# A delta-rule block for the latents alone with unsplit float32 operands, the context still in high and low parts

## The chip, the cores and the metric

The kernel runs on one core of a Trainium2 chip. The metric is device time in microseconds of one execution, the median of several runs. The core's engines are TensorE (PE, matmuls; its weight loads are listed as PEld), VectorE (DVE), ScalarE (ACT), GpSimd (POOL) and SyncE (SP), whose queue issues nearly all DMAs. A core works with one on-chip memory of 128 partitions (SBUF) and with accumulators (PSUM) in banks of 512 float32 columns.

## The reference

Two blocks run on 256 tokens of width 1024 (x). The first mixes stick-breaking attention with a state-space branch, then attends to a memory, then applies a convolutional feed-forward layer. The second has two layers; each is a mixer followed by a mixture of 32 experts. The mixer of its first layer is the one of this case, a gated delta rule that runs in both directions, with 8 heads of 128:

```
p = h @ w_in                      # h = modulate(x) of the latents, or of the context (256 tokens)
q, k, v = split(silu(conv3(p[:, :3072])));  z = p[:, 3072:4096]
beta = sigmoid(p[:, 4096:4112]);  g = -exp(a_log) * softplus(p[:, 4112:] + dt_bias)
per chunk of 64 tokens:           # u, w solve a unit lower triangular system built from k, beta, g
    v_new = u - w @ S;  o = q_dec @ S + (q k^T * decay) @ v_new;  S = S * g_last + k_dec^T @ v_new
y = (norm(o) * silu(z)) @ w_out   # the latents' scan starts from the context's final S
```

The context needs only its final states S, so it has no q and no z. h is a norm: x times its inverse root mean square, times a column of scales, plus a column of shifts. All inputs and the output are float32.

## The kernel before

Activations are kept transposed, features on partitions and the 256 tokens in the free dimension, as 8 slices of 128 features. A weight tile is 1 MB (128 x 2048 float32) and holds 256 output columns for all 8 slices, so two output blocks of 128 columns. `wload` (line 312) loads it on the SP queue into a ring of five.

Matmuls of the dense projections are made of three products in a faster float32 form that rounds its operands (F32R). `split` (line 321) turns half a weight tile into a high part (ScalarE copy, line 325) and a low part (subtract, line 327, on VectorE, or on GpSimd where a share says so; the shares of the latents' queries, values and gates say GpSimd every time, that of the keys VectorE). There are two buffers for such pairs (`wsp`). The activation h is kept as a high and a low part as well (hh, hl). `mm3` (line 330) issues high x high, high x low and low x high. `gemm_t` (line 336) does this for all blocks of a projection: 24 matmuls a block, and then an `evac` that empties the bank. Attention scores (line 835), the recurrence, the expert layers and the transposes use plain float32 operands with no split.

`mod_t` (line 941) makes h: squares on ScalarE, the inverse root on VectorE or GpSimd, two matmuls a slice with a diagonal of it (line 504, transposing), then per slice an affine step on VectorE (952), a ScalarE copy to hh (953) and a VectorE subtract to hl (954).

The class `Delta` holds the steps for the context (dc) and for the latents (dl). `decays` (1030) projects beta and g from a 128 x 8 x 32 weight that is loaded and split once near the start (lines 1486 to 1491), and builds masks on GpSimd and VectorE. `keys` (1138), `values` (1173) and `queries` (1192) are projections with a convolution on VectorE (`conv3`, 993, its steps at lines 997, 998 and 1002) behind each block. `chunks` (1205) forms k k^T, sends it through DRAM to regroup it, inverts 32 x 32 triangles in a loop of 31 x 2 dependent VectorE operations (1237, 1239), sends the result through DRAM again and joins the parts with small matmuls (1264, 1275). `steps` (1300) is the recurrence: four steps of matmuls and VectorE updates. The gates z (1635) are projected in two halves, the second of them behind the recurrence (`Z_LATE`), and the output projection `wa_out` follows, then the experts.

The order of the work is written by generators. `weave` (239) runs several of them beside one another, the latents (1583), the context (1399), queries, values and gates (1616), the two `decays`, and the modulation weights of line 910; each `yield` gives a cost in planned microseconds, and the generator with the least planned time goes on. The framework then orders each engine's instructions by priority and by a timeline of its own; on the chip each engine, and the SP queue, works strictly in that order.

Of the kernel before, what the change touches and what calls it, by code (L numbers as in the profile page):

```python
# [12 lines left out]
F32R = mybir.dt.float32r  # L13
# [194 lines left out]
def tile_blocks(ctx: ExitStack, tc: tile.TileContext, A, out):  # L208
# [121 lines left out]
    def mm3(ps, ah, al, bh, bl, start, stop):  # L330
# [2 lines left out]
        PE.matmul(ps, ah, bl, start=False, stop=False)  # L333
        PE.matmul(ps, al, bh, start=False, stop=stop)  # L334

    def gemm_t(name, tiles, kt, h, evac, share=None):


        hh, hl = h
        late = None  # L340
        ncols = WT // kt
        cb = 1024 // (kt * P)
        blk = 0
        for i in tiles:
            w3 = wload(name, i).rearrange("p (k n) -> p k n", n=ncols)
            for n0 in range(0, ncols // P, cb):
                h3, l3 = split(w3[:, :, n0 * P:(n0 + cb) * P], (kt, cb * P), SHARES.get(name, 0) if share is None else share)
                for j in range(cb):
                    ps = bank()[:, :T]
                    for k in range(kt):  # L350
                        mm3(ps, h3[:, k, j * P:(j + 1) * P], l3[:, k, j * P:(j + 1) * P], hh[:, k], hl[:, k],
                            k == 0, k == kt - 1)
                    later = evac(blk, ps)
                    if late:
                        late()
                    late = later if callable(later) else None
                    blk += 1
                yield 2.6
        if late:
            late()  # L360

    def gemm_n(name, i, ncols, h, pss, k0, klast):


        hh, hl = h
        nh = ncols // 512
        w2 = wload(name, i).rearrange("p (k n) -> p k n", n=ncols)
        kc = 2 // nh
        for ka in range(0, WT // ncols, kc):
            h3, l3 = split(w2[:, ka:ka + kc], (kc, ncols), SHARES.get(name, 0))  # L370
            for k in range(kc):
                kk = k0 + ka + k
                for t in range(2):
                    ah, al = hh(kk, t), hl(kk, t)
                    for n in range(nh):
                        sl = slice(n * 512, (n + 1) * 512)
                        PE.matmul(pss[t][n], ah, h3[:, k, sl], start=kk == 0, stop=False)
                        PE.matmul(pss[t][n], ah, l3[:, k, sl], start=False, stop=False)
                        PE.matmul(pss[t][n], al, h3[:, k, sl], start=False, stop=kk == klast)  # L379
            yield 2.6  # L380

    def gemm_out(name, h, nh=2, evac=None):


        f = [lambda k, t, q=q: q[:, k, t * P:(t + 1) * P] for q in h]
        pss = [[None] * nh, [None] * nh]
        for n in range(nh):
            if evac and n and n == nh - 1:
# [11 lines left out]
        for c in range(2):  # L400
            ps = [bank("acc")[:, :256] for t in range(2)]
            for kq in range(2):
                h3, l3 = split(ws[kq][:, :, c * 256:(c + 1) * 256], (4, 256), SHARES.get(name, 0))
                for k in range(4):
                    for t in range(2):
                        kk = 4 * kq + k
                        ah, al = f[0](kk, t), f[1](kk, t)
                        PE.matmul(ps[t], ah, h3[:, k], start=kk == 0, stop=False)
                        PE.matmul(ps[t], ah, l3[:, k], start=False, stop=False)
                        PE.matmul(ps[t], al, h3[:, k], start=False, stop=kk == 7)  # L410
                yield 2.6
# [529 lines left out]
    def mod_t(src, a, b, E=G, wait=6, mark=None):  # L941

        with urgent():
            dg = diagonals(rms(src, E))
        hh = big("hh", (8, T), F32R)
        hl = big("hl", (8, T), F32R)
        have[mark] = True
        yield wait
        for k in range(8):
            ps = transposed(src, dg, k)  # L950
            t = temp()
# [4 lines left out]
        return hh, hl  # L956

    def gated_into(x, gb, router):

# [53 lines left out]
    class Delta:  # L1013
# [16 lines left out]
        def decays(self):  # L1030
            yield from until(("h", self.live))
            use(*DECB)
            hh, hl = self.h
            dth = self.dth
            E = G if DEC_POOL & (2 if self.live else 1) else V
            M = G if MASK_POOL & (2 if self.live else 1) else V
            pb = bank()
            for k in range(8):
                mm3(pb[:32, :T], wsh[:, k], wsl[:, k], hh[:, k], hl[:, k], k == 0, k == 7)
            bs = temp()[:32]  # L1040
            for t in range(2):
                S.activation(bs[:, t * P:(t + 1) * P].rearrange("p (c j) -> p c j", j=64), in_tile(pb[:32, :T], t), AF.Copy)
# [440 lines left out]
    nexp = const.tile([P, 16], F32, name="nexp")  # L1483
    exp_cols(nexp, rows32[:, 0:16], 16)
    V.tensor_scalar(nexp, nexp, -1.0, None, op0=OP.mult)
    wsm = temp().rearrange("p (k n) -> p k n", n=32)
    nc.sync.dma_start(wsm, A["wa_s"])
    wsh = const.tile([P, 8, 32], F32R, name="wsh")
    wsl = const.tile([P, 8, 32], F32R, name="wsl")
    S.activation(wsh, wsm, AF.Copy)  # L1490
    V.tensor_tensor(wsl, wsm, wsh, op=OP.subtract)

    class ExpertWeights:


# [87 lines left out]
    def latents():  # L1583
        yield from first()
        have["ffn"] = True
        use("mm", "acc", "fb", "acc")
        dl.h = yield from mod_t(x, scale_col("norm_mix0", ada_c0, 1, 0), ada_c0[:, 0, :, 0], V if RS_V & 4 else G, WAIT3, "x3")
        have["h", True] = True
        use(*KEYB)
        yield from dl.keys()  # L1590
# [411 lines left out]
```

## Time and profile before

| | |
|---|---|
| median of 3 runs | 2170.59 us (2167.99 to 2180.1) |
| the profiled execution | 2169.38 us |
| its span, first to last instruction | 2167.6 us, 31109 instructions |
| mean granted TensorE clock | 0.964 of full speed |
| delta rule of the latents | about 713 to 990 us of the span |

The profile is one execution. A page gives each engine's busy time, queries give stretches, lines and single instructions in order of time. Times of rows are microseconds from the start of the span unless marked ns. A matmul's own duration includes the way through the array, so the cost of one in a series is read from the distance of the starts.

### The profile page before, as it was taken

How to read it: one execution, taken by the hardware profiler on the slowest of the kernel's cores; microseconds unless marked ns; L12 is line 12 of the kernel's file. 1: busy time of each engine (PE TensorE's matmuls, PEld its weight loads, DVE VectorE, ACT ScalarE, POOL GpSimd, SP SyncE). 2: the span in 40 equal slices, each digit the busy share in tenths (PEclk: the TensorE clock that was granted, in tenths of full speed). 3: DMA queues.
4: the chain of work that ended last, by engine and by line, in shares of the span. 5: the costliest groups of instructions: out<-in, count | busy, mean ns of one | idle time of the engine just before them, and what ended most of it. 6: DMA issues, size and time to landing. Idle time of an engine off the chain costs nothing. (4 is left out here: it accounts for less than half of the span.)

```text
span 2167.6 us, 31109 instructions
## 1 busy us (share of the span) xinstructions
PE 1976.3 (91%) x12476; PEld 1269.3 (59%) x12476; DVE 1107.4 (51%) x2277; ACT 652.4 (30%) x1236; POOL 289.0 (13%) x444
## 2 busy tenths in 40 slices
PE   5999999989999889898999989898798999999996
PEld 5778787789988767777434333333596333333332
DVE  6797377867966587666333222222565332222223
ACT  4325655555645332543111011110342111111101
POOL 6484001110000374320000000000000000000000
PEclk8999999999999888998999999999898999999999
DMA  6533355536555235548799999997754999999992
GB/s 260 195 114 120 137 214 185 214 128 219 198 173 203 101 139 182 182 176 332 281 420 419 419 413 386 404 373 286 294 203 179 408 420 419 420 384 418 419 391 98
DMA packets 103508, 592.08 MB, mean 273 GB/s; under 512 B 30272, under 2 KB 30656, under 8 KB 32704
## 3 DMA queue, kind: packets, MB, share of 16 engines
q1 hardware_dynamic: 103216, 589.52, 69.6%
q8 instruction: 100, 1.64, 0.3%
q10 hardware_dynamic: 144, 0.52, 0.1%
q14 instruction: 48, 0.39, 0.0%
HBM read 585.81 MB, written 4.19 MB: 272 GB/s over the span
## 5 line engine op out<-in xcount | busy, mean ns | idle before, releaser
L327 DVE TENSOR_TENSOR whl<-w,whl 128x1024 fp32r<-128x1024 f32 x210 | 267.0, 1272 | 123.8 <-ACT whl L325 122.1
L1802 PE MATMUL acc<-wa,xq 128*64 128x512 f32 x1152 | 311.7, 599 | 2.6 <-DVEq L1873 2.6
L325 ACT ACTIVATE whl<-w 128x1024 fp32r<-128x1024 f32 x236 | 248.2, 1054 | 168.3 <-PE acc L379 72.8
L332 PE MATMUL mm<-hh,whl 128*128 128x256 f32 x912 | 264.9, 291 | 15.7 <-DVE hl L524 5.3
L334 PE MATMUL mm<-hh,whl 128*128 128x256 f32 x912 | 264.2, 290 | 1.5 <-DVE whl L327 1.3
L333 PE MATMUL mm<-hl,whl 128*128 128x256 f32 x912 | 260.9, 286 | 0.0
L332 PEld LDWEIGHTS mm<-hh,whl 128*128 128x128 f32 x912 | 177.0, 194 | 24.5 <-issue 7.3
L1802 PEld LDWEIGHTS acc<-wa,xq 128*64 128x64 f32 x1152 | 93.2, 137 | 163.3 <-issue 156.3
L334 PEld LDWEIGHTS mm<-hh,whl 128*128 128x128 f32 x912 | 177.0, 194 | 10.9 <-issue 4.4
L1802 PE MATMUL acc<-w,xq 128*64 128x512 f32 x640 | 182.8, 597 | 0.0
L333 PEld LDWEIGHTS mm<-hl,whl 128*128 128x128 f32 x912 | 176.9, 194 | 1.2 <-issue 0.4
L1841 DVE TENSOR_TENSOR acc<-acc,gb 128x512 f32<-128x512 f32 x64 | 44.7, 699 | 172.0 <-PE acc L1837 144.2
L1849 DVE TENSOR_TENSOR x<-x,mm 128x512 f32<-128x512 f32 x128 | 82.3, 683 | 95.8 <-PE mm L1848 95.8
L1802 PEld LDWEIGHTS acc<-w,xq 128*64 128x64 f32 x640 | 54.3, 137 | 86.8 <-issue 83.2
L1783 DVE TENSOR_SCALAR xq<-mm,scnorm_ffn,ada_c 128x256 f32<-128x256 f32 x64 | 34.4, 543 | 128.2 <-PE mm L1781 67.6
L332 PE MATMUL acc<-hh,whl 128*128 128x256 f32 x288 | 86.7, 301 | 4.5 <-DVE x L547 3.8
L334 PE MATMUL acc<-hh,whl 128*128 128x256 f32 x288 | 84.9, 295 | 0.3 <-DVE whl L327 0.2
L1784 ACT ACTIVATE xq<-mm,ada_c,scnorm_ffn 128x256 f32<-128x256 f32 x64 | 35.6, 563 | 161.9 <-DVE xq L1783 154.4
L1695 POOL MEMSET t2b<- 128x512 f32 x1 | 0.5, 524 | 627.9 <-PE fb L1570 627.9
L333 PE MATMUL acc<-hl,whl 128*128 128x256 f32 x288 | 84.2, 292 | 0.0
L327 POOL TENSOR_TENSOR whl<-w,whl 128x1024 fp32r<-128x1024 f32 x26 | 62.6, 2412 | 129.0 <-ACT whl L325 64.9
L1837 PE MATMUL acc<-wa,t2a 128*64 128x512 f32 x288 | 77.7, 598 | 2.3 <-ACT t2a L1827 1.2
(796 smaller groups left out, 3852.1 us busy)
## 6 DMA issues: line engine op xcount, KB each, us to landing
wa<-in_w_dram SPq DMA_DIRECT2D x216, 1024.0 KB, 10.5
w<-in_w_dram SPq DMA_DIRECT2D x120, 1024.0 KB, 9.5
w<-in_ada_w_dram SPq DMA_DIRECT2D x48, 1024.0 KB, 4.9
ww<-in_w_dram SPq DMA_DIRECT2D x48, 1024.0 KB, 10.4
w<-in_w_up_dram SPq DMA_DIRECT2D x22, 1024.0 KB, 4.8
w<-in_wa_kv_dram SPq DMA_DIRECT2D x16, 1024.0 KB, 4.9
w<-in_wb_in_dram SPq DMA_DIRECT2D x12, 1024.0 KB, 4.8
w<-in_w_down_dram SPq DMA_DIRECT2D x11, 1024.0 KB, 4.9
```

The costliest lines, as they stand in the source:

```text
L325: S.activation(h3, src, AF.Copy)
L327: (G if share and nsplit[0] % share == 0 else V).tensor_tensor(l3, src, h3, op=OP.subtract)
L332: PE.matmul(ps, ah, bh, start=start, stop=False)
L333: PE.matmul(ps, ah, bl, start=False, stop=False)
L334: PE.matmul(ps, al, bh, start=False, stop=stop)
L1695: G.memset(beats, 0.0)
L1783: V.tensor_scalar(xt[:, k0], ps[:, 0], a[:, k0:k0 + 1], b[:, k0:k0 + 1], op0=OP.mult, op1=OP.add)
L1784: S.activation(xt[:, k0 + 1], ps[:, 1], AF.Identity, scale=a[:, k0 + 1:k0 + 2], bias=b[:, k0 + 1:k0 + 2])
L1802: PE.matmul(ph[i][sl], xt[:, 4 * kq + k, s0 + 64 * e:s0 + 64 * e + 64], w[e][:, k * 512:(k + 1) * 512], start=kq == 0 and k == 0, stop=kq ...
L1837: PE.matmul(py[c][sl], ht[:, f, sl], w[e][:, f * 512:(f + 1) * 512], start=f == 0, stop=f == 3, tile_position=(0, 64 * e))
L1841: V.tensor_tensor(py[c][:m], py[c][:m], gb[:m, cs], op=OP.mult)
L1849: V.tensor_tensor(x[:, t, cs], x[:, t, cs], pa, op=OP.add)
```

## The change

For the latents alone, h stays one float32 tensor `hf`, written from the transposing matmul by VectorE and ScalarE in turn; `gemm_t` gets whole operands and issues 8 plain float32 matmuls a block with the weight as loaded, no split. Keys, values, queries and gates of the latents take this way, and their decays. The context keeps hh and hl and its split weights. The small decay weight is loaded inside each `decays` (for the context it is split there). `gemm_n` and `gemm_out` get the same branch, which nothing here takes: the output projection keeps its split. In the planned order a step of an unsplit projection counts 3.4 instead of 2.6, a slice of the norm 0.8 instead of 1.

```diff
+    def whole(h):
+        return not isinstance(h, (tuple, list))
 def gemm_t(name, tiles, kt, h, evac, share=None):
         for i in tiles:
             w3 = wload(name, i).rearrange("p (k n) -> p k n", n=ncols)
+            if whole(h):
+                for j in range(ncols // P):
+                    ps = bank()[:, :T]
+                    for k in range(kt):
+                        PE.matmul(ps, w3[:, k, j * P:(j + 1) * P], h[:, k], start=k == 0, stop=k == kt - 1)
+                    later = evac(blk, ps)
+                    if late:
+                        late()
+                    late = later if callable(later) else None
+                    blk += 1
+                    if (j + 1) % cb == 0:
+                        yield 3.4
+                continue
+            hh, hl = h
...
 def mod_t(src, a, b, E=G, wait=6, mark=None, exact=False):
+        if exact:
+            hf = big("hf", (8, T))
...
         for k in range(8):
             ps = transposed(src, dg, k)
+            if exact:
+                if k % 2:
+                    V.tensor_scalar(hf[:, k], ps, a[:, k:k + 1], b[:, k:k + 1], op0=OP.mult, op1=OP.add)
+                else:
+                    S.activation(hf[:, k], ps, AF.Identity, scale=a[:, k:k + 1], bias=b[:, k:k + 1])
+                yield 0.8
+                continue
...
 def decays(self):
+            wsm = temp().rearrange("p (k n) -> p k n", n=32)
+            nc.sync.dma_start(wsm, A["wa_s"])
+            if not self.live:
+                wsh, wsl = temp(F32R).rearrange("p (k n) -> p k n", n=32), temp(F32R).rearrange("p (k n) -> p k n", n=32)
+                S.activation(wsh, wsm, AF.Copy)
+                V.tensor_tensor(wsl, wsm, wsh, op=OP.subtract)
             for k in range(8):
-                mm3(pb[:32, :T], wsh[:, k], wsl[:, k], hh[:, k], hl[:, k], k == 0, k == 7)
+                if self.live:
+                    PE.matmul(pb[:32, :T], wsm[:, k], self.h[:, k], start=k == 0, stop=k == 7)
+                else:
+                    mm3(pb[:32, :T], wsh[:, k], wsl[:, k], self.h[0][:, k], self.h[1][:, k], k == 0, k == 7)
...
-    wsm = temp().rearrange("p (k n) -> p k n", n=32)
-    nc.sync.dma_start(wsm, A["wa_s"])
-    wsh = const.tile([P, 8, 32], F32R, name="wsh")
-    wsl = const.tile([P, 8, 32], F32R, name="wsl")
-    S.activation(wsh, wsm, AF.Copy)
-    V.tensor_tensor(wsl, wsm, wsh, op=OP.subtract)
...
-        dl.h = yield from mod_t(x, scale_col("norm_mix0", ada_c0, 1, 0), ada_c0[:, 0, :, 0], V if RS_V & 4 else G, WAIT3, "x3")
+        dl.h = yield from mod_t(x, scale_col("norm_mix0", ada_c0, 1, 0), ada_c0[:, 0, :, 0], V if RS_V & 4 else G, WAIT3, "x3", True)
```

## Rows read from the trace of the kernel before

**Rows 1.** The page's totals: busy us (share of the span) xinstructions.
```profile
PE 1976.3 (91%) x12476; PEld 1269.3 (59%) x12476; DVE 1107.4 (51%) x2277; ACT 652.4 (30%) x1236; POOL 289.0 (13%) x444
```
**Rows 2.** Stretches: from:to length, busy PE PEld DVE ACT POOL (x), clock, DMA, GB/s.
```profile
735.00:798.00 63.00, 63.00 (x543) 51.61 (x532) 51.67 (x140) 27.62 (x72) 43.36 (x104) 0.95 0.46 170
798.00:840.00 42.00, 34.31 (x289) 28.58 (x286) 29.23 (x70) 11.12 (x19) 26.75 (x33) 0.84 0.48 150
840.00:882.00 42.00, 36.11 (x311) 29.02 (x310) 39.88 (x104) 15.50 (x34) 12.77 (x6) 0.92 0.52 186
882.00:914.00 32.00, 27.55 (x432) 25.92 (x430) 14.05 (x29) 15.78 (x31) 13.90 (x6) 0.95 0.71 212
914.00:965.00 51.00, 51.00 (x676) 39.67 (x674) 33.94 (x103) 22.04 (x71) 7.94 (x5) 1.00 0.48 187
...
1050.00:1500.00 450.00, 417.71 (x1946) 161.89 (x1942) 126.72 (x223) 51.75 (x90) 0.00 (x0) 1.00 0.98 405
```
**Rows 3.** Timeline of TensorE, 690 to 1000: start, us, line, out<-in, count.
```profile
689.98 0.28 PE L332 MATMUL mm<-hh,whl 128*128 128x256 f32 x1
...
692.86 0.28 PE L332 MATMUL mm<-hh,whl 128*128 128x256 f32 x1
...
733.95 1.92 PE L910 MATMUL fb<-w,cst 128*32 128x512 f32 x16
```
**Rows 4.** Line 835 (count, duration ns min/median/max, first and last start, forms).
```profile
L835 PE MATMUL acc<-kx,qx x32: 378/379/382, 407.0 to 417.3; 128*128 128x256 f32 x32
```
**Rows 5.** Timeline of TensorE, 407 to 418.
```profile
407.05 3.62 PE L835 MATMUL acc<-kx,qx 128*128 128x256 f32 x16
410.50 0.60 PE L917 MATMUL fb<-ident,t2b 128*128 128x128 f32 x4
```
**Rows 6.** Groups by line, 713 to 990: busy, mean ns, idle before.
```profile
L327 POOL TENSOR_TENSOR whl<-w,whl 128x1024 fp32r<-128x1024 f32 x25 | 60.3, 2414 | 98.6 <-ACT whl L325 64.9 <-PE mm L1390 30.9 <-issue 2.7
...
L327 DVE TENSOR_TENSOR whl<-w,whl 128x1024 fp32r<-128x1024 f32 x7 | 10.8, 1540 | 0.5 <-ACT whl L325 0.5
...
L325 ACT ACTIVATE whl<-w 128x1024 fp32r<-128x1024 f32 x32 | 33.5, 1051 | 4.0 <-DMA w<-in_wa_q_dram 2.7 <-DMA w<-in_wa_z_dram 1.3
```
**Rows 7.** Timeline of GpSimd, 840 to 900.
```profile
863.79 2.41 POOL L327 TENSOR_TENSOR whl<-w,whl 128x1024 fp32r<-128x1024 f32 x1 [2.40 <-ACT whl L325]
```
**Rows 8.** Timeline of VectorE, 840 to 900: first, two inner and last inverse steps.
```profile
840.82 0.20 DVE L1237 TENSOR_TENSOR t1a<-inva 128x31 f32<-128x31 f32 x1 [3.14 <-DMA inva<-da]
...
862.25 0.42 DVE L1239 TENSOR_TENSOR inva<-inva,t1a 128x252 f32<-128x252 f32 x1
...
863.88 2.59 DVE L1239 TENSOR_TENSOR inva<-inva,t1a 128x247 f32<-128x247 f32 x1
...
881.50 0.19 DVE L1239 TENSOR_TENSOR inva<-inva,t1a 128x31 f32<-128x31 f32 x1
```
**Rows 9.** Timeline of VectorE, 713 to 735, the norm.
```profile
726.59 0.54 DVE L952 TENSOR_SCALAR t1a<-acc,scnorm_mix,ada_c 128x256 f32<-128x256 f32 x1
...
728.41 0.76 DVE L954 TENSOR_TENSOR hl<-t1a,hh 128x256 fp32r<-128x256 f32 x2 [0.94 <-ACT hh L953]
```
**Rows 10.** Timeline of TensorE, 796 to 812: the wait stands in brackets.
```profile
806.53 1.97 PE L1352 MATMUL fb<-t2b,ti 64*64 64x128 f32 x16 [5.50 <-DVE t2b L1344]
...
809.16 3.35 PE L910 MATMUL fb<-w,cst 128*32 128x512 f32 x16
```
**Rows 11.** Timeline of VectorE, 793 to 807.
```profile
793.87 1.99 DVE L1307 TENSOR_TENSOR dm<-dec,m 128x16 f32<-128x16 f32 x1
...
800.72 2.88 DVE L1314 COPY se<-eg 64x16 f32<-64x16 f32 x4
```
**Rows 12.** Timeline of VectorE, 968 to 992.
```profile
973.20 2.23 DVE L1608 TENSOR_TENSOR sso<-sso,so 128x16 f32<-128x16 f32 x1 [0.82 <-ACT t1a L1604]
...
980.64 3.38 DVE L327 TENSOR_TENSOR whl<-w,whl 128x1024 fp32r<-128x1024 f32 x1
```
**Rows 13.** DMA issues of the whole span: count, KB each, median us to landing.
```profile
t1a<-in_wa_s_dram SPq DMA_DIRECT2D x1, 128.0 KB, 11.1
```

More of the change, by code (lines that the diff above doesn't have):

```diff
@@ L334, in mm3 @@
         PE.matmul(ps, al, bh, start=False, stop=stop)
+    def whole(h):
+        return not isinstance(h, (tuple, list))
     def gemm_t(name, tiles, kt, h, evac, share=None):
-        hh, hl = h
         late = None
@@ L362, in gemm_n @@
     def gemm_n(name, i, ncols, h, pss, k0, klast):
-        hh, hl = h
         nh = ncols // 512
@@ L368, in gemm_n @@
         kc = 2 // nh
+        if whole(h):
+            for k in range(WT // ncols):
+                kk = k0 + k
+                for t in range(2):
+                    for n in range(nh):
+                        PE.matmul(pss[t][n], h(kk, t), w2[:, k, n * 512:(n + 1) * 512], start=kk == 0, stop=kk == klast)
+                if (k + 1) % kc == 0:
+                    yield 3.4
+            return
+        hh, hl = h
         for ka in range(0, WT // ncols, kc):
@@ L382, in gemm_out @@
     def gemm_out(name, h, nh=2, evac=None):
-        f = [lambda k, t, q=q: q[:, k, t * P:(t + 1) * P] for q in h]
+        if whole(h):
+            f = lambda k, t: h[:, k, t * P:(t + 1) * P]
+        else:
+            f = [lambda k, t, q=q: q[:, k, t * P:(t + 1) * P] for q in h]
         pss = [[None] * nh, [None] * nh]
@@ L402, in gemm_out @@
             for kq in range(2):
+                if whole(h):
+                    for k in range(4):
+                        for t in range(2):
+                            kk = 4 * kq + k
+                            PE.matmul(ps[t], f(kk, t), ws[kq][:, k, c * 256:(c + 1) * 256], start=kk == 0, stop=kk == 7)
+                    yield 3.4
+                    continue
                 h3, l3 = split(ws[kq][:, :, c * 256:(c + 1) * 256], (4, 256), SHARES.get(name, 0))
@@ L939, in scale_col, with mod_t @@
         return a
-    def mod_t(src, a, b, E=G, wait=6, mark=None):
+    def mod_t(src, a, b, E=G, wait=6, mark=None, exact=False):
         with urgent():
             dg = diagonals(rms(src, E))
-        hh = big("hh", (8, T), F32R)
-        hl = big("hl", (8, T), F32R)
+        if exact:
+            hf = big("hf", (8, T))
+        else:
+            hh = big("hh", (8, T), F32R)
+            hl = big("hl", (8, T), F32R)
         have[mark] = True
@@ L950, in mod_t @@
             ps = transposed(src, dg, k)
+            if exact:
+                if k % 2:
+                    V.tensor_scalar(hf[:, k], ps, a[:, k:k + 1], b[:, k:k + 1], op0=OP.mult, op1=OP.add)
+                else:
+                    S.activation(hf[:, k], ps, AF.Identity, scale=a[:, k:k + 1], bias=b[:, k:k + 1])
+                yield 0.8
+                continue
             t = temp()
@@ L955, in mod_t @@
             yield 1
-        return hh, hl
+        return hf if exact else (hh, hl)
     def gated_into(x, gb, router):
@@ L1032, in decays @@
             use(*DECB)
-            hh, hl = self.h
             dth = self.dth
@@ L1036, in decays @@
             M = G if MASK_POOL & (2 if self.live else 1) else V
+            wsm = temp().rearrange("p (k n) -> p k n", n=32)
[4 more added lines that the diff above has]
+                V.tensor_tensor(wsl, wsm, wsh, op=OP.subtract)
             pb = bank()
             for k in range(8):
-                mm3(pb[:32, :T], wsh[:, k], wsl[:, k], hh[:, k], hl[:, k], k == 0, k == 7)
+                if self.live:
+                    PE.matmul(pb[:32, :T], wsm[:, k], self.h[:, k], start=k == 0, stop=k == 7)
+                else:
+                    mm3(pb[:32, :T], wsh[:, k], wsl[:, k], self.h[0][:, k], self.h[1][:, k], k == 0, k == 7)
             bs = temp()[:32]
```

## The prediction

> **What bounds the kernel now.** I read the page's totals first, then one table of stretches, then single engines inside the stretch that the change touches. The totals [rows 1] show TensorE busy 91% of the span and VectorE 51%, but a share over the whole span says nothing of one stage. The table [rows 2] does. From 1050 to 1500 us (the first expert stage) the DMA engines are 0.98 busy at 405 GB/s: that stage lasts as long as its weights take to arrive, starts when the work before it is done, and so passes a shift on one to one. I assume the same of what follows it. The change acts before, from 713 us (norm of the latents) to 990 us (output projection of the delta rule). There TensorE reads 63.00 of 63 and 51.00 of 51 us in two stretches, yet 34.31 of 42, 36.11 of 42 and 27.55 of 32 in the three between, while VectorE has 39.88 of 42 in 840 to 882. The reader is to see two kinds of stretch: those packed with matmuls, where each microsecond added to TensorE is lost, and 798 to 914, where TensorE waits and a VectorE chain (the triangular inverses, 62 dependent operations at lines 1237 and 1239) sets the pace.
>
> **TensorE pays more.** A block here is one 128-column output block of a projection: 24 matmuls of split operands, at lines 332 to 334. Two of them 24 apart start at 689.98 and 692.86 [rows 3], so a block takes 2.88 us, 0.120 a matmul. The unsplit form stands at line 835: plain float32, 128x128 stationary, 256 columns, just the shape that is added. Its trace has 32 records [rows 4] for 16 matmuls in the code (four heads, two tiles, two k), so a float32 matmul leaves two records. Sixteen records run from 407.05 to the next start at 410.50 [rows 5]: 0.216 us each, 0.431 a matmul. A block of 8 takes 3.45 us, 0.57 more than before. Keys, values, queries and gates have 8 blocks each: 32 x 0.57 = 18.2 us. The decays have 32 stationary columns; no row shows float32 at this shape. At line 835's price they go from at most 24 x 0.120 = 2.88 to 3.45, +0.57; at one pass each they would take 8 x 0.120 = 0.96, a gain of 1.9. I take the nearer row, +0.6, and leave both ends in the range. TensorE thus gets 19 us more.
>
> The Trainium skill would price this step higher: "FP8 and Floating Point Precision", section "TensorE Precision Notes", counts four passes for true float32, and "TensorE: Matmul & The Clock Gate", section "Back-to-back issue gap", gives 256/2.4 + 2.5 = 109 ns a pass. By them a block would go from 24 x 0.109 = 2.62 to 32 x 0.109 = 3.49 us, +0.87, and the sum over 32 blocks would be 28 us. The four passes agree with 0.431 [rows 5], the 0.109 does not agree with the 0.120 [rows 3].
>
> **The other engines get time back.** In 713 to 990 the splits of these weights are 24 of the 25 on GpSimd at 2.41 us (values, queries, gates), six on VectorE for the keys (two more ran before) at 1.23 us ((7 x 1.540 - 3.38)/6, without the one of [rows 12]), and 32 on ScalarE at 1.05 us [rows 6]; one or two rows belong to the output projection and stay. The larger return is indirect. While GpSimd runs a split, VectorE operations that read SBUF stand still: the split from 863.79 to 866.20 [rows 7] lies on a VectorE subtract that takes 2.59 us, where its neighbour of almost the same size takes 0.42 [rows 8]. In the stretch of the inverse loop there are five such, from 843.6 to 875.8, each 1.7 to 2.2 us above the time of its neighbours: 10.1 us.
>
> **The sum, stage by stage.**
> (a) Norm. Today each slice needs a VectorE affine step, a ScalarE copy and a VectorE subtract; the last subtract ends at 728.41 + 0.76 = 729.2, the last affine step at 726.59 + 0.54 = 727.1 [rows 9]. One affine step is left, on two engines in turn; I take 0.54 for either. With no subtracts ahead of it in the queue the last ends near 726.4 (an estimate: 727.1 less two of the subtracts, 0.76 together), 2.8 us sooner; the 0.6 of the decays comes behind it. -2.3, bounds 0 and -4.
> (b) Keys and first two query blocks, 735 to 798. TensorE is contiguous; nine blocks lie here: 9 x 0.57 = +5.1. VectorE gives back 5 x 1.23 = 6.2 us, but TensorE shows no gap for it; I take 2 of it, nearer to the rows of TensorE. +3.1, bounds -1.1 and +5.1.
> (c) 798 to 840. TensorE waits 5.50 us for a VectorE step of the context's recurrence [rows 10]. Ahead of that step stand small operations that splits hold up: line 1307 takes 1.99 and the four at line 1314 take 2.88 [rows 11], where a step of this size takes 0.2 [rows 8]: 1.8 + 2.1 = 3.9 us. The next weight product of line 910 then runs below full clock (the stretch has 0.84 [rows 2]), 3.35 us [rows 10] against the 1.92 of the same form at 733.95 [rows 3]: 1.4 more. Against it six query blocks, +3.4. -1.9, bounds +3.4 and -5.3.
> (d) The inverses, 840 to 882. -10.1; the five blocks inside lie under the VectorE chain. Without that cover they would cost 2.9. Bounds -4 and -11.
> (e) 882 to 914. From the last inverse step at 881.50 [rows 8] the result goes to DRAM and back. Nothing in this trip changes. Eight blocks of values and gates lie here, +4.6, half of them under the trip: +2.3, bounds 0 and +4.6.
> (f) The recurrence, 914 to 965, keeps its instructions: 0, if no more gate blocks land in it than today (none).
> (g) End, 965 to 990. Line 1608 takes 2.23 instead of 0.2, and line 327 3.38 instead of 1.23 [rows 12], with the last gate step behind it: both lie under GpSimd splits of the gates. -4.2, against it +0.7 for four gate blocks that now fill today's waits. -3.5, bounds 0 and -6.
> (h) The context keeps its splits, but the small decay weight (128 KB) is now loaded at each use, and its split of about 1 us follows the load. Ahead of the context's decays nothing hides it but the queue's lead. A load of this tensor took 11.1 us [rows 13]; SP works in order, and behind it stand weight loads that are mostly early. +1, bounds 0 and +11. For the latents the load lies under the norm.
> Sum: -2.3 + 3.1 - 1.9 - 10.1 + 2.3 + 0 - 3.5 + 1 = -11.4. The profiled execution took 2169.4 us (2167.6 of span, 1.8 around it), 1.2 below the median of the three runs; 2169.4 - 11.4 gives 2158.
>
> A weight tile now goes back to the ring when its last matmul has read it, not after its split, up to one block (3.45 us) later. The loads still lead by four tiles, so I count nothing; if that cover is gone, the landing of a tile shows as a TensorE gap. The order of the emitted work also shifts: a block counts 3.4 units in it instead of 2.6.
>
> **Rivals.**
> *TensorE is the bound all along.* Every added 19 us is paid and the VectorE time returned becomes waiting; only (a) stays: 2169.4 + 19 - 2.3 = 2186. It decides once no stretch between 735 and 990 has a TensorE gap. For it: the two full stretches. Against it: 18.0 us in which TensorE is idle in 798 to 914 (7.7 + 5.9 + 4.4 [rows 2]), the longest wait of them for VectorE [rows 10]. 0.16.
> *The gates slip into the recurrence.* Values end later than the inverses in the emitted order, so the four gate blocks that fill the trip today land in 914 to 965, where TensorE is full: 4 x 3.45 = 13.8. 2158 + 13.8 - 2.3 of (e) = 2170, no change. For it: values are emitted 6.4 units later per projection. Against: TensorE is idle in the trip if they don't run there. 0.27.
> *VectorE is the bound in (b) too.* Then 6.2 instead of 2 comes back; with (c) at its lower end: 2158 - 4.2 - 3.4 = 2150. For it: 51.67 of 63 us VectorE busy there. Against it: 63.00 of 63 on TensorE. 0.17.
> *The pages' price.* 0.30 a block more than my rows on 32 blocks, all on the path: 2158 + 9.6 = 2168; 0.02, for its 0.109 is not what the trace has.
> That the change doesn't do what it says (an unsplit matmul that is no slower) is excluded by the shape of line 835.
>
> **How the numbers follow.** Forecast 2158: 0.38. A measurement of this kernel tells apart about 0.5%, 11 us either way. My forecast lies just beyond that edge (12.6 below the median), so I give 0.28 of it, and all of the 0.17 at 2150, to faster, with 0.03 of the slip coming out lower: 0.48. Slower are the TensorE bound's 0.16 and 0.02 of the slip: 0.18. The rest, 0.34, is no change. One case in ten left out at either end gives 2141 to 2183; the forecast's own range is 2149 to 2168.
>
> **What would show it.** Blocks of 16 records over 3.45 us; no GpSimd split but the output projection's one or two; inverse loop near 31 us from first to last step instead of 40.7; no 5.5 us TensorE gap ahead of line 1352; line 1608 near 0.2 us. I am wrong if the loop stays near 40 us, if TensorE has gate blocks between the recurrence's steps, or if the context's decays show a gap over 5 us.

## The result and the profile after

The changed kernel takes 2143.7 us (median of four runs, 2141.7 to 2149.0) against 2171.7 for the kernel before (2168.0 to 2180.1): ratio 0.9875, 95% interval 0.9856 to 0.9893, 28 us faster. The forecast was 2158 us, a gain of 11.4 in its sum; the time lies inside the range of 2141 to 2183. The size is more than twice the forecast's, and the experiments show that this is two things: 12 to 15 us that the change makes ahead of the experts, close to the sum, and the rest from an order of instructions inside the expert stages that the change does not touch.

The profiled execution of the changed kernel took 2142.1 us, 2140.3 of them span. The rows that answer to [rows 1] (the page's totals: busy us, share, instructions):

```profile
PE 1980.2 (93%) x12212; PEld 1256.9 (59%) x12212; DVE 1060.3 (50%) x2258; ACT 623.2 (29%) x1200; POOL 216.9 (10%) x419
```

TensorE is 3.9 us busier than in [rows 1] although 264 instructions fewer are on it, GpSimd 72 us less busy. Next come the stretches of the delta rule, as in [rows 2], but cut at events: norm of the latents, transposes of their decays, 798 us, first and last step of the inverse loop, first product of queries and state, last output of the recurrence, last slice for the output projection, first expert matmul.

```profile
core 0: us, PE busy (x) PEld busy (x) DVE busy (x) ACT busy (x) POOL busy (x), PEclk, DMA share, GB/s
716.30:742.30 26.00, 26.00 (x161) 18.94 (x162) 5.22 (x15) 6.53 (x14) 0.00 (x0) 0.92 0.23 84
742.30:798.00 55.70, 54.09 (x366) 41.58 (x366) 37.23 (x119) 16.66 (x57) 35.90 (x118) 1.00 0.40 151
798.00:826.60 28.60, 28.42 (x255) 22.97 (x252) 18.24 (x54) 4.78 (x10) 7.21 (x9) 1.00 0.59 185
826.60:860.60 34.00, 33.37 (x229) 25.11 (x231) 32.97 (x119) 8.64 (x22) 0.00 (x0) 0.95 0.59 217
860.60:891.70 31.10, 31.10 (x417) 22.48 (x411) 13.22 (x34) 14.48 (x33) 0.00 (x0) 1.00 0.74 221
891.70:960.40 68.70, 68.70 (x734) 54.94 (x731) 36.93 (x109) 24.36 (x84) 5.07 (x4) 1.00 0.45 174
960.40:978.80 18.40, 16.12 (x87) 13.53 (x86) 12.12 (x35) 8.39 (x38) 0.01 (x1) 1.00 0.51 191
978.80:1022.00 43.20, 32.95 (x216) 29.39 (x214) 24.98 (x85) 14.56 (x27) 2.90 (x2) 0.84 0.83 336
```

Where [rows 2] had TensorE idle for 18 us between 798 and 914, it now has work in all but 0.2, 0.6 and 0.0 us of the three stretches from 798 to 891.7. The same stretch from the norm to the first expert matmul in one row, first of the kernel before, then of the changed one:

```profile
713.90:1038.10 324.20, 290.65 (x2708) 244.81 (x2710) 221.65 (x581) 127.23 (x317) 117.03 (x157) 0.89 0.51 183
```

```profile
716.30:1022.00 305.70, 290.74 (x2446) 228.92 (x2446) 180.91 (x565) 98.40 (x283) 51.09 (x132) 0.96 0.54 196
```

The 18.5 us that the stretch lost are TensorE's idle time: 33.6 before, 15.0 after. Its busy time is the same to 0.1 us, although the change adds work that I priced at 19 us; the granted clock, a mean over its two levels of 1.2 and 2.4 GHz (1.00 is the higher), rose from 0.89 to 0.96. In [rows 2] it was lowest, 0.84, where TensorE waited longest; it is 1.00 in five of the eight rows above. Busy time times clock, an estimate of the work in us of the higher level, goes from 290.65 x 0.89 = 259 to 290.74 x 0.96 = 279: the 20 more are close to what I had priced, and the clock paid for them. Not all of its rise is the change's, as (a) below shows.

The same two traces, cut at events (us from the event of one row to that of the next, the first from the start of the span; the letters are those of the forecast):

| from ... to | before | after | difference | forecast |
|---|---|---|---|---|
| start ... diagonals of the latents' norm (h) | 713.9 | 716.3 | +2.4 | +1 |
| ... last slice of the norm (a) | 15.3 | 8.5 | -6.8 | -2.3 |
| ... first query block written (b) | 69.3 | 74.9 | +5.6 | +3.1 |
| ... decay matrices issued to DRAM (c) | 32.9 | 15.3 | -17.6 | -1.9 |
| ... first inverse step | 9.4 | 11.6 | +2.2 | none |
| inverse loop (d) | 40.9 | 34.0 | -6.9 | -10.1 |
| ... first product of queries and state (e) | 33.4 | 31.1 | -2.3 | +2.3 |
| recurrence (f) | 52.3 | 68.7 | +16.4 | 0 |
| ... last slice for the output projection (g) | 24.8 | 18.4 | -6.4 | -3.5 |
| ... first expert matmul | 45.9 | 43.2 | -2.7 | none |
| first expert stage, to its last hidden tile | 481.5 | 468.9 | -12.6 | 0 |
| ... output issued to DRAM | 643.7 | 645.2 | +1.5 | 0 |

Up to the first expert matmul the change gains 16.1 us. The rest is in the first expert stage, whose matmuls and loads are the same in both kernels. There the weight loads run 16 us ahead of those of before up to 1188 us and 29 us ahead at 1450, in five steps of about 2.4 us and one of 1.5. One such step in TensorE's timeline of the kernel before (L1837 the down projection of a pair of experts, L1848 its additions into x, waits in brackets):

```profile
1211.03 0.73 PE L1848 MATMUL mm<-t2b,t1a 128*128 128x512 f32 x2 [0.66 <-ACT t2b L1843]
1211.75 0.73 PE L1848 MATMUL mm<-t2a,t1a 128*128 128x512 f32 x2
1212.42 3.22 PE L1837 MATMUL acc<-wa,t2a 128*64 128x512 f32 x13
1215.47 0.59 PE L1837 MATMUL acc<-wa,t2a 128*64 128x512 f32 x1
1217.49 0.73 PE L1848 MATMUL mm<-t2b,t1a 128*128 128x512 f32 x2 [1.42 <-ACT t2b L1843]
```

and the same pair in the changed kernel (L1884, L1895):

```profile
1189.70 7.09 PE L1884 MATMUL acc<-wa,t2a 128*64 128x512 f32 x32
1196.71 0.73 PE L1895 MATMUL mm<-t2b,t1b 128*128 128x512 f32 x2
1197.28 0.62 PE L1895 MATMUL mm<-t2a,t1b 128*128 128x512 f32 x2
1197.84 1.07 PE L1849 MATMUL acc<-wa,xq 128*64 128x512 f32 x2
1198.84 0.74 PE L1895 MATMUL mm<-t2b,t1b 128*128 128x512 f32 x2
```

The reader is to see that the first additions stand in the middle of the down projection before, where they wait for a ScalarE cast twice (0.66 and 1.42 us), and behind it after, where they wait for nothing. Nobody wrote this order: the framework's timeline gives it pair by pair. Up to its last hidden tile the first stage has nine pairs in the waiting order before, four after; the second stage is alike in both.

### The profile page after: what moved, and what is told of

It reads as the page before. It is cut to its first block, busy times and chain, and to the rows that moved or that the text cites. A ratio compares the mean times of both kernels' runs of the same rounds, so it can differ in the third digit from the quotient of the medians.

```text
span 2140.3 us, 30475 instructions
## 1 busy us (share of the span) xinstructions
PE 1980.2 (93%) x12212; PEld 1256.9 (59%) x12212; DVE 1060.3 (50%) x2258; ACT 623.2 (29%) x1200; POOL 216.9 (10%) x419
## 3 DMA queue, kind: packets, MB, share of 16 engines
q8 instruction: 98, 1.61, 0.3%
## 5 line engine op out<-in xcount | busy, mean ns | idle before, releaser
L327 DVE TENSOR_TENSOR whl<-w,whl 128x1024 fp32r<-128x1024 f32 x203 | 255.2, 1258 | 111.7 <-ACT whl L325 109.9
L325 ACT ACTIVATE whl<-w 128x1024 fp32r<-128x1024 f32 x204 | 214.7, 1054 | 154.4 <-PE acc L405 71.0
L332 PE MATMUL mm<-hh,whl 128*128 128x256 f32 x736 | 215.1, 292 | 12.0 <-DVE hl L560 5.5
L334 PE MATMUL mm<-hh,whl 128*128 128x256 f32 x736 | 215.0, 292 | 2.0 <-DVE whl L327 1.9
L333 PE MATMUL mm<-hl,whl 128*128 128x256 f32 x736 | 212.3, 288 | 0.0
L332 PEld LDWEIGHTS mm<-hh,whl 128*128 128x128 f32 x736 | 145.2, 197 | 18.2 <-DVE hl L560 6.2
L334 PEld LDWEIGHTS mm<-hh,whl 128*128 128x128 f32 x736 | 144.9, 197 | 9.0 <-issue 4.0
L333 PEld LDWEIGHTS mm<-hl,whl 128*128 128x128 f32 x736 | 145.3, 197 | 1.3 <-issue 0.8
L353 PE MATMUL mm<-hf,w 128*128 128x256 f32 x352 | 82.8, 384 | 1.9 <-DVE sz L1680 1.9
L1884 PE MATMUL acc<-wa,t2b 128*64 128x512 f32 x288 | 74.5, 597 | 2.3 <-ACT t2b L1874 1.2
L1884 PE MATMUL acc<-wa,t2a 128*64 128x512 f32 x288 | 72.4, 596 | 2.3 <-ACT t2a L1874 1.2
L353 PEld LDWEIGHTS mm<-hf,w 128*128 128x128 f32 x352 | 64.5, 190 | 14.9 <-issue 2.4
L332 PE MATMUL acc<-hh,whl 128*128 128x256 f32 x224 | 66.0, 295 | 6.3 <-DVE x L583 5.6
L334 PE MATMUL acc<-hh,whl 128*128 128x256 f32 x224 | 65.2, 291 | 0.4 <-DVE whl L327 0.2
## 6 DMA issues: line engine op xcount, KB each, us to landing
w<-in_w_dram SPq DMA_DIRECT2D x120, 1024.0 KB, 11.4
```

Of the source, the lines that this page charges most:

```text
L325: S.activation(h3, src, AF.Copy)
L327: (G if share and nsplit[0] % share == 0 else V).tensor_tensor(l3, src, h3, op=OP.subtract)
L332: PE.matmul(ps, ah, bh, start=start, stop=False)
L353: PE.matmul(ps, w3[:, k, j * P:(j + 1) * P], h[:, k], start=k == 0, stop=k == kt - 1)
L1884: PE.matmul(py[c][sl], ht[:, f, sl], w[e][:, f * 512:(f + 1) * 512], start=f == 0, stop=f == 3, tile_position=(0, 64 * e))
```

## The experiments

All ran beside the kernel before, whose medians beside them were 2171.9 (runs 1 to 4), 2169.2 (5 to 8), 2170.0 (9 to 11) and 2172.0 us (12). "Down first" below is the edit of the first run.

**1. The kernel before, additions behind the down projection.**

```
-    PE.matmul(py[c][sl], ht[:, f, sl], w[e][...], ...)
+    down = PE.matmul(py[c][sl], ht[:, f, sl], w[e][...], ...)
...
+    with tc.issue_after(down.ins):
         for q in (yh_, yl_):
             PE.matmul(pa, selw[:m, t * P:(t + 1) * P], q[:m], ...)
```

> The kernel before with one thing changed: in the two expert stages each pair's additions into x come behind both halves of its down projection on TensorE, an order that the framework's planned times give or don't give pair by pair. In the kernel before, pairs of the first expert stage have seven down-projection matmuls behind the first additions, and TensorE waits there for a ScalarE cast (0.66 and 1.42 us in one pair); after the change five of these pairs have the other order, and each of the five is 2.3 us shorter. Theory (the planned order made the 12.6 us that the first expert stage gained): the first expert stage, 481.5 us before from its first matmul to the last hidden tile, falls to 469 or below (nine such pairs at up to 2.3 us: about 461), the second from 497 to about 481, total 2171.7 to about 2136 (2130 to 2160). Rival (the stage's length is the weight transfers' own and varied by itself): both stages stay within 3 us and the total at 2169 to 2174.

Measured: 2122.5 us (2122.1 to 2127.4), ratio 0.9778 (0.9764 to 0.9792): 49 us faster, more than expected. The first expert stage takes 457.7 us instead of 481.5, the second, counted to the output's issue, 476.9 instead of 497.0. The theory stands, its price per pair was too small. That is more than the change itself brought, without touching the delta rule.

**2. The changed kernel with the same edit.**

> The changed kernel with the same order of the expert stages as in the first run. Theory: the four pairs of the first and seven of the second expert stage that still wait lose about 2.3 us each: 2143.7 to about 2118, and against the first run only what the change does ahead of the experts is left: 16 us shorter (the start of the expert stage moved from 1038.1 to 1022.0), 0.7 to 0.8 percent. Rival (the expert stage gained for a reason of its own in the changed kernel, such as an earlier start of its weights): the difference between the two stays at 28 us.

Measured: 2109.9 us (2105.4 to 2113.5), ratio 0.9711 (0.9694 to 0.9727), 8 us below what was expected. With one order in both, the first expert matmul comes at 1024.3 against 1039.0 us, the expert stage's gain of 12.6 is gone (460.4 against 457.7), and the two medians stand 12.7 us apart. That is what the change does by itself. All later runs but the eighth carry this edit.

**3. GpSimd's work put back.**

```
     for j in range(ncols // P):
+        if share:
+            z = view(wsp.tile([P, WT], F32R, name="whl", tag="W"), 1024, (kt, P))
+            G.tensor_tensor(z, w3[:, :, j * P:(j + 1) * P], w3[:, :, j * P:(j + 1) * P], op=OP.subtract)
         ps = bank()[:, :T]
```

> The second run with one GpSimd subtract of 128x1024 put back for each block of queries, values and gates (24 of them, from the landed weight into a scratch tile that nobody reads); the matmuls stay unsplit float32. Theory (GpSimd's splits held up VectorE, TensorE waited for VectorE, and its clock fell in the waits): the inverse loop goes from 34 back to about 41 us, TensorE waits of 10 us or more come back between 800 and 900, and the total rises by 8 to 18 us over the second run. Rival (what counted was the chain from weight to split to matmul, or the order, and not the hold-up): the total rises by 3 us or less.

Measured: 2135.2 us (2130.3 to 2140.3), 25.3 above the second run and more than either theory expected. The inverse loop takes 46.7 us instead of 34.0. Its last steps on VectorE:

```profile
881.97 0.21 DVE L1294 TENSOR_TENSOR t1a<-inva 128x60 f32<-128x60 f32 x1
882.22 1.86 DVE L1296 TENSOR_TENSOR inva<-inva,t1a 128x60 f32<-128x60 f32 x1
884.12 1.78 DVE L1294 TENSOR_TENSOR t1a<-inva 128x31 f32<-128x31 f32 x1
885.94 0.19 DVE L1296 TENSOR_TENSOR inva<-inva,t1a 128x31 f32<-128x31 f32 x1
```

and GpSimd's two subtracts over the two slow ones:

```profile
882.12 3.74 POOL L353 TENSOR_TENSOR whl<-w 128x1024 fp32r<-128x1024 f32 x2 [4.34 <-DMA w<-in_wa_kv_dram]
```

Nobody reads what GpSimd writes here, so no wait on data explains it: 1.86 beside 0.21 us. The Trainium skill states this in "SBUF — State Buffer", section "SBUF: two separate sides": VectorE and GpSimd share a port pair; a GpSimd instruction, or a VectorE operation with two SBUF inputs while GpSimd reads SBUF, holds it for the whole instruction if it starts first, and the other blocks. The trace agrees: the steps have two SBUF inputs. From the norm to the first expert matmul, second run first, then this one:

```profile
717.60:1024.30 306.70, 290.49 (x2444) 228.25 (x2446) 181.07 (x565) 98.52 (x283) 51.37 (x132) 0.97 0.54 196
```

```profile
719.10:1052.90 333.80, 303.45 (x2445) 237.35 (x2446) 202.76 (x564) 98.75 (x283) 97.10 (x156) 0.92 0.50 180
```

The hold-up is paid twice: TensorE idles 30.4 instead of 16.2 us, and the same matmuls take 13.0 us more, with the granted clock at 0.92 instead of 0.97. Some 2.1 of the 13.0 lie in the norm, ahead of the first of these subtracts (775.7 us). That GpSimd now reads the weight tiles as well is not what TensorE waits for: none of its waits in the row ends on the landing of a tile, and the one that grew most, from 0.8 to 5.3 us, ends on VectorE's convolution of the queries.

**4. A ninth matmul in each unsplit block.**

```
+    PE.matmul(ps, w3[:, 0, j * P:(j + 1) * P], h[:, 0], start=True, stop=True)
     for k in range(kt):
```

> The second run with one more float32 matmul in each of the 32 unsplit blocks (the first one is issued twice): 32 x 0.43 = 13.8 us more TensorE work, nothing else. Theory (since the change TensorE is full from 742 to 960 and is the bound there): 12 to 14 us more. Rival (VectorE's inverse chain still sets the pace where about nine of the blocks lie): 7 to 10 us more. If TensorE had slack everywhere: under 3.

Measured: 2127.1 us (2121.8 to 2128.1), 17.2 more for 13.8 of work, above the theory's 12 to 14. Work added to TensorE is paid in full after the change; nothing covers its blocks any more. The excess was not taken apart; the norm, with a later rise of the clock, takes 10.7 us instead of 8.3, and the trip of the inverses through DRAM, from the last step to the first product, is 19.3 us here and 12.9 in the second run.

**5 to 7. The context's weight, the planned costs, the place of the gates.**

```
5: for the context wa_s loaded and split once ahead of the second weave
6: -    yield 3.4      +    yield 2.6        (norm: 0.8 -> 1)
7: -Z_LATE = 2         +Z_LATE = 4
```

> The second run (changed kernel, additions behind the down projections) with the context's decay weight loaded and split once ahead of the second weave, as the kernel before has it; the latents still load theirs at use. Theory (the load at use delays the context's decays and with them the small stages around 346 us): the latents' norm starts 2 to 3 us earlier (717.6 to about 715), and the total falls by as much, to about 2107. Rival (the 2.5 us come from the order that the framework plans, not from the load): within 2 us of 2110 either way.

> The second run with the planned costs of before: a step of an unsplit projection counts 2.6 instead of 3.4, a slice of the norm 1 instead of 0.8. Theory (TensorE is full from 742 to 960, so where its blocks are planned matters little): total within 4 us of 2110. Rival (the gate blocks between the steps of the recurrence cost their 13.8 us, and the larger cost put them there): gates 1 to 4 go back ahead of the recurrence and the total falls by 8 to 14 us.

> The second run with all eight gate blocks emitted behind the recurrence instead of four. Theory (TensorE full): the recurrence, 68.7 us from its first product of queries and state to its last output, shortens by up to 13.8 us and the stretch behind it grows by as much, total within 4 us of 2110. Rival (gate blocks are what fills the recurrence's own waits): the recurrence shortens by less than 7 us and the total rises by 7 us or more. Other side (gates between the steps hold up the recurrence): total falls by 5 us or more.

Measured: 2110.2 us (ratio 0.9728, 0.9709 to 0.9748), 2105.7 (0.9702, 0.9683 to 0.9721) and 2106.6 (0.9704, 0.9685 to 0.9724); all three intervals overlap that of the second run; the sixth lies 0.3 us outside its theory. In the fifth the norm starts 2.6 us earlier, as expected, but the first expert matmul only 1.1: the theory holds for the start and fails for the total. In the sixth, gates 1 to 3 end before the recurrence starts and gate 4 just behind its start; the recurrence takes 53.2 us, and the inverse loop starts 14 us later in exchange. In the seventh the recurrence takes 56.2 instead of 68.7 us, and the total falls by no more than the intervals allow. The first expert matmul comes at 1026.9 and 1029.1 us, against 1024.3 in the second run; without the norm and its start, which differ by the clock, the stretch is 2.2 us shorter and 2.9 us longer. Where a full TensorE has its gate blocks makes little difference.

**8. The kernel before, splits on VectorE instead of GpSimd.**

```
-QSHARE = 1      +QSHARE = 0     (VSHARE and ZSHARE likewise)
```

> A look at the kernel before with the splits of queries, values and gates on VectorE instead of GpSimd; expert stages as in the kernel before; all matmuls split as before. Read by the start of the expert stage (1038.1 us before, 1022.0 after the change). Theory (GpSimd's port hold-up on VectorE was the cost): 24 splits x 1.23 us come to VectorE, but the holds of 1.7 to 2.2 us go and GpSimd's own 2.41 us go from each block's chain; the inverse loop falls from 40.9 to 35 to 38 us and the expert stage starts 5 to 12 us earlier. Rival (VectorE's load is what bounds, whoever causes it): the expert stage starts within 3 us of 1038 or later.

Measured: 2160.8 us (one run); the first expert matmul at 1024.9 instead of 1038.1, 13.2 earlier. The expectation for the loop fails: it takes 51.0 us, with nine splits among its steps,

```profile
L327 DVE TENSOR_TENSOR whl<-w,whl 128x1024 fp32r<-128x1024 f32 x9 | 11.0, 1218 | 0.0
L1239 DVE TENSOR_TENSOR inva<-inva,t1a 128x31 f32<-128x31 f32 (+15 forms) x31 | 10.5, 339 | 0.4
```

but no step is held up any more (339 ns a step, against 444 in the third run), the loop starts 11.4 us earlier, and the values, which the recurrence needs as well, end 17.0 us earlier.

**9. The eighth run's edit with down first.**

> The first run (split operands everywhere, additions behind the down projections) with the splits of queries, values and gates on VectorE instead of GpSimd: the eighth run showed an expert stage 13 us earlier from this alone. Theory (the change gains what it takes from GpSimd, and unsplit float32 itself gains nothing): 2122.5 falls to 2108 to 2114, level with the second run at 2109.9 within 5 us. Rival (the unsplit form adds a gain of its own, the ScalarE and VectorE time of the splits): 2116 or more, at least 6 us above the second run.

Measured: 2108.4 us (2103.9 to 2110.5), ratio 0.9708 (0.9695 to 0.9721), level with the second run. Its row from the norm to the first expert matmul:

```profile
716.50:1023.60 307.10, 278.37 (x2708) 237.58 (x2710) 216.38 (x606) 129.04 (x317) 65.18 (x133) 0.92 0.52 193
```

The split form needs 12.1 us less of TensorE than the second run, though at a lower clock (0.92 against 0.97), and waits 12.5 us more (28.7 against 16.2). So unsplit float32 gains nothing over split operands once GpSimd is out of the way; what the change gains is what it takes from GpSimd.

**10. The second write of the inverses on another queue.**

```
-nc.sync.dma_start(db, src)
+(nc.scalar if src is ivt and live else nc.sync).dma_start(db, src)
...
(the reads of the second write likewise)
```

> The first run with the DRAM trip of the latents' inverses divided: the second write (the transposed inverses) and the reads of it go out on ScalarE's DMA queue, the first write and its reads stay on SP's. In the first run, as in the kernel before, the framework puts a 1 MB weight load between the two writes on SP's queue, and the second write lands 8.5 us after its issue, against 3.0 us in the changed kernel, where the load comes behind both. Theory (the second write waits for the weight load ahead of it on its queue): the second write lands about 3 us after its issue, the trip from the last inverse step to the first off-diagonal product falls from 20.6 to 13 to 15 us, and the total by 3 to 7 us. Rival (the transfers share the DMA engines, whichever queue they come from): the trip stays at 18 us or more, total within 2 us of 2122.5.

Issue to landing of the second write: the kernel before, the changed kernel, this run (name, queue, count, KB, median us):

```profile
db<-inva SPq DMA_DIRECT2D x1, 512.0 KB, 8.5
```

```profile
db<-inva SPq DMA_DIRECT2D x1, 512.0 KB, 3.0
```

```profile
db<-inva ACTq DMA_DIRECT2D x1, 512.0 KB, 8.2
```

The rival holds for the transfer: 8.2 us from ScalarE's queue too, behind a weight load issued 2.0 us earlier on SP. The Trainium skill says in "DMA: Bandwidth & Descriptors", section "Issuing engines are not separate DMA queues", that DMAs of different engines run on the same 16 DMA engines and interleave. The trace agrees in this, that the other queue is no way past the load. The total rose to 2129.4 us, 6.9 above the first run, which neither expected: ScalarE waits to issue the reads, issues them, and computes nothing for 7.06 us,

```profile
898.18 0.47 ACT L996 ACTIVATE t1a<-mm,cols 128x256 f32<-128x256 f32 x1 [7.06 <-issue]
```

and TensorE waits 9.24 us for a value block that stands behind it (3.30 in the first run).

**11 and 12. Looking for a better version.** The eleventh run takes the edits of 5, 6 and 7 together; the twelfth splits keys and queries again (on ScalarE and VectorE), with the norm writing both forms.

```
12: -yield from gemm_t("wa_q", range(4), 8, self.h, ...)
    +yield from gemm_t("wa_q", range(4), 8, self.hs, ...)      (keys likewise; QSHARE = 0)
```

> The second run with the context's decay weight early, the old planned costs and all gate blocks behind the recurrence together (fifth, sixth and seventh run). Theory (each moved work about on a TensorE that is full, and the 3 to 4 us of the sixth and seventh run are order): 2102 to 2108, no better than the best of them by more than 3 us. Rival (each is a gain of its own): 2099 or below.

> The second run with keys and queries split again (ScalarE and VectorE, none on GpSimd; the norm writes the float32 tensor and its hi and lo), values, gates and decays unsplit. Keys and queries lie where TensorE was full in both kernels (735 to 826 us), values and gates beside the inverse loop. Theory (TensorE is the bound in 742 to 826 and VectorE has slack there, 37 of 56 us busy): 16 x 0.57 = 9.1 us of TensorE come off, 16 VectorE splits of 1.23 us lie beside it, the norm grows by up to 3 us: 4 to 8 us less, 2102 to 2106. Rival (with the splits VectorE is full there, or the longer norm eats it): 2108 to 2114.

Measured: 2112.0 us (0.9738, 0.9725 to 0.9751) and 2111.7 (0.9728, 0.9706 to 0.9750). Neither beats the second run. The eleventh lies above its theory's 2108 too: the differences of 5 to 7 do not add up. In the twelfth the theory falls. Its row from the norm to the first expert matmul,

```profile
718.10:1029.20 311.10, 289.82 (x2574) 233.85 (x2575) 199.84 (x587) 115.32 (x305) 62.07 (x132) 0.94 0.52 190
```

shows where the 9.1 us went: TensorE idles 21.3 us instead of 16.2 and its clock is 0.94 instead of 0.97, so that it is busy for 289.8 us, only 0.7 less. The fastest versions, at 2106 to 2112 us, all have down first and no split on GpSimd in the delta rule's queries, values and gates, with unsplit float32 or (run 9) without.

## Why the prediction came out as it did

**The direction and the size ahead of the experts were right.** The sum was -11.4 us; the change by itself brings -12.7 (runs 1 and 2), -14.7 at the first expert matmul. GpSimd's hold-up of VectorE was the right cause: run 3 puts it back and loses 25.3 us, run 9 takes it away without the new number format and is level with run 2. That the measured time lies inside the range at all, 2.7 us above its lower end, is luck: the expert stage's 12.6 us stood in no term.

**The assumption that failed is "passes a shift on one to one".** The work ahead passed its 16.1 us on, and the expert stage added 12.6 of its own. I read that stage as bound by its transfers alone, from a DMA share of 0.98 [rows 2]. The missing 0.02 and the 405 GB/s, where its best 50 us stretches have 420, were the sign: the loads were late where TensorE waited. Run 1 shows that the order cost this time; that a waiting TensorE delays the loads because it holds their slots is read from the steps of 2.4 us and was not tested by itself.

**Inside the sum, most terms were wrong one by one and right together,** since they describe positions on a TensorE that becomes full. That the misses cancel to within 1.3 us is in part luck.
(a) The norm gave 6.8 us, outside its bounds of 0 and -4, but most of that is the clock. Norm to last slice, in the kernel before, in run 1 and in the changed kernel:

```profile
713.90:729.20 15.30, 15.30 (x72) 13.80 (x73) 6.75 (x16) 4.66 (x12) 0.00 (x0) 0.58 0.00 0
```

```profile
717.50:728.40 10.90, 10.90 (x72) 9.81 (x73) 6.45 (x16) 4.50 (x12) 0.00 (x0) 0.85 0.00 0
```

```profile
716.30:724.80 8.50, 8.50 (x46) 7.43 (x47) 2.03 (x5) 2.53 (x5) 0.00 (x0) 0.74 0.00 0
```

Run 1 has the norm of the kernel before, with the same 72 matmul records, and takes 4.4 us less: the lower clock level ends 12.8 us into the norm before (0.50 from 713.9 to 726.7), 3.4 us into it in run 1. Run 1 does not have the change, and runs 4, 6 and 7, which have it, take 10.7, 13.5 and 11.4 us with the clock rising later; why it rises when it does was not taken apart. The change's own part is the other 2.4 us, near the forecast: the slices now leave on two engines in turn, seven of the eight ending within 1.5 us (VectorE's four):

```profile
721.38 1.45 DVE L992 TENSOR_SCALAR hf<-acc,scnorm_mix,ada_c 128x256 f32<-128x256 f32 x3 [5.05 <-PE acc L540]
724.21 0.55 DVE L992 TENSOR_SCALAR hf<-acc,scnorm_mix,ada_c 128x256 f32<-128x256 f32 x1 [1.38 <-PE acc L540]
```

(b) +5.6 against +3.1, just past its upper bound of +5.1: as if the added blocks were paid in full where TensorE was full, though not quite the same work lies in the stretch in both kernels. A block costs what [rows 5] gave, 3.55 us from 900.16 to the next start instead of 3.45, and the decays with their 32 columns cost the nearer row's price, 3.58 from start to start, not the 0.96 of one pass a matmul:

```profile
735.13 3.64 PE L1091 MATMUL mm<-hf,t1a 128*32 128x256 f32 x16
738.71 0.43 PE L1394 MATMUL fb<-states,kT 128*64 128x128 f32 x2
...
900.16 3.62 PE L353 MATMUL mm<-hf,w 128*128 128x256 f32 x16
903.71 0.82 PE L1430 MATMUL acc<-t2a,kt 64*128 64x128 f32 x5
```

Against the 2.88 of [rows 3] a block thus costs 0.67 more, where I had 0.57 and the rival with the higher price 0.87.
(c) -17.6 against -1.9, bounds exceeded. The 5.50 us wait of [rows 10] is gone, as forecast (the longest TensorE wait from 742 to 826 is 1.61), and with it the low clock of the stretch (0.84 to 1.00). The larger part is order: the planner now puts the inverses' inputs ahead of the later query blocks, which run beside the loop. With the old planned costs (run 6) the same term comes back, and the total does not rise.
(d) -6.9 against -10.1, inside the bounds. No step waits for GpSimd any more, and one of the two lines falls from 18.7 us to 10.6 (the row before, the two after):

```profile
L1239 DVE TENSOR_TENSOR inva<-inva,t1a 128x31 f32<-128x31 f32 (+15 forms) x31 | 18.7, 603 | 0.6
```

```profile
L1293 DVE TENSOR_TENSOR inva<-inva,t1a 128x31 f32<-128x31 f32 (+15 forms) x31 | 10.6, 341 | 0.6
L1291 DVE TENSOR_TENSOR t1a<-inva 128x31 f32<-128x31 f32 (+15 forms) x31 | 10.5, 338 | 5.8 <-DMA inva<-da 5.4
```

But more of the other work lies between the steps: VectorE is busy for 32.97 of the loop's 34.0 us, and the steps make only 21.1 of them.
(e) -2.3 against +2.3, below its lower bound of 0. "Nothing in this trip changes" was false: a weight load stood between its two writes on SP's queue before, and behind both after, and the second write landed in 3.0 instead of 8.5 us. That the load's place is the cause is read from the traces; run 10 only shows that another queue does not help, and moving the load alone was not tried. The first write, ahead of that load, was slower before as well (4.5 against 2.7 us), so loads issued earlier may have a part.
(f) The rival did happen here, and with it a sign that I had named of being wrong: gate blocks lie between the steps of the recurrence, which grew by 16.4 us (the rival said 13.8). But it did not cost: runs 6 and 7 take them out again for 4.2 and 3.2 us, within the intervals, and do not reach the first expert matmul earlier. I had priced a moved block and forgotten that the place it leaves becomes shorter.
(g) -6.4 against -3.5, just past the lower bound. The signs are there: line 1608, now 1655, takes 0.18 us instead of 2.23 [rows 12].
(h) +2.4 against +1, within the bounds, and run 5, whose norm starts 2.6 us earlier, shows that it is worth nothing at the end. That the load is its cause is not shown: run 1, which loads this weight as the kernel before does, starts its norm at 717.5. No gap over 5 us stands ahead of the context's decays.

**The rivals.** TensorE as the bound all along: work added to it is paid in full now (run 4), though work taken off it gains nothing (run 12); before the change it was not the bound, since run 9 has the matmuls of run 1 and is 14.1 us faster. VectorE as the bound in (b): no, the stretch became longer. The slip came, without its price. A TensorE gap that ends on the landing of a weight tile, as I feared of tiles held longer, does not show in the changed kernel's stretch from 742 to 960.

**What I had not priced at all is the clock.** I counted it once, 1.4 us in (c). Over the whole stretch it went from 0.89 to 0.96, TensorE's busy time stayed at 290.7 us with 19 us of work added (it rose by 3.7, from 286.8 to 290.5, between runs 1 and 2, whose norms have the early rise of the clock in common), and in run 3 it makes 13.0 of the 27.1 us.

## What to carry to other kernels

A split or copy that moves to GpSimd to relieve VectorE can cost more than it relieves: look in the trace for VectorE operations several times as long as their neighbours and for a GpSimd instruction over them, and try the work on VectorE first; here that alone was worth as much as the change of the number format. Where one engine becomes full, sum its work, its idle time and its clock over the whole stretch; terms that price positions cancel. And compare the order of the instructions of stages that a change does not touch, since a planner may write them anew: here two matmul groups in the wrong order cost 49 us, more than the change gained.

## What the runs showed of the hardware

A GpSimd subtract whose result nobody reads lengthens a 0.2 us VectorE operation with two SBUF inputs to 1.8 us (run 3). A float32 matmul with 32 stationary columns costs as much as one with 128 (3.58 and 3.55 us for eight). A 512 KB write behind a 1 MB load lands after 8.2 to 8.5 us from SP's queue or ScalarE's, after 3.0 us with no load ahead, and reads that ScalarE issues, which wait for such a write, hold up ScalarE's own work (7.06 us in run 10). The same matmuls took 290.5 us at a granted clock of 0.97 and 303.5 us at 0.92, and the same norm 10.9 us at 0.85 and 15.3 us at 0.58.
